# Twelve of sixteen token tiles transposed by VectorE and DRAM instead of TensorE, with the norm's gain folded into the gate's weights

## The chip, the cores and the metric

One core of one Trainium2 chip. The metric is the device time of one execution in microseconds, the median over the runs; lower is better. The kernel is a single launch on that core.

## What is computed

A pre-norm encoder layer over 2048 tokens of width 1024, in float32: an mLSTM mixer, a squared-ReLU MLP, then the part that this change touches, a gated per-token embedding, and a last norm.

```python
h = h + mix                                            # mLSTM mixer
h = h + sqrelu_mlp(rmsnorm(h, norm_mlp[i]), mlp_w1[i], mlp_w2[i])
gate = sigmoid(rmsnorm(h, norm_ple[i]) @ ple_gate_w[i] + ple_gate_b[i])
h = h + gate * (p[i] @ ple_w[i])                       # p: 2048 x 256
return rmsnorm(h, norm_final)

def rmsnorm(x, gain):
    return x * rsqrt(mean(x * x, axis=-1) + EPS) * gain
```

The norm's gain multiplies columns of h, so it may as well multiply rows of the gate's weights; the reciprocal root is one number per token, so it may as well multiply the gate's product afterwards.

## The kernel before

A product in float32 is made of three matmuls: each operand is split into a rounded part (`hi`, type fp32r) and the rest (`lo`), and `mm3` adds hi*hi, hi*lo and lo*hi in one PSUM bank. ScalarE makes `hi` by a cast, VectorE makes `lo` by a subtraction (`split`). The weights are split once, by `Weight.prep`.

The mixer and the MLP's two products fill the first 2170 us (the MLP by seven products in place of eight on 2x2 blocks; banks `pa`, `pb`, `pc`). The MLP's second product adds its results to the residual `h1_d` in DRAM by accumulating DMAs on POOL's queue. The last part takes the 2048 tokens as 16 tiles of 128, numbered 0 to 15 here. For each tile `Tok`:

- `load` brings the tile's 128x1024 residual (`h2`) on SP's queue, four tiles ahead. The residuals of tiles 2 and up lie in a ring of seven buffers (`Ot`), so the load of tile t+7 waits until tile t has been written out.
- `norm` sums squares on ScalarE, makes the reciprocal root (`rstd`: ScalarE's log and exp, then one Newton step of VectorE) and scales the tile by it and by the gain's row `row_ple` (VectorE, 128x1024, result `xs`).
- `tr0` and `tr1` transpose half a tile each: four 128x128 transposes on TensorE into the one PSUM bank `pt`, then `split` into `xTh` and `xTl`.
- `half` does half of the output columns, twice: 24 gate matmuls into `pg` (8 blocks of the width, three each), 6 matmuls of the embedding into `pl`, then bias, sigmoid, product, residual add and sum of squares.
- `fin` makes the last norm and writes the tile out, on POOL's queue (the last two tiles on SP's and ScalarE's).

The embedding `p` already takes another way to its transposed form, before the last part: VectorE transposes 32x32 blocks (`shuffle`), four POOL DMAs write the blocks to DRAM in an order (`p_d`) from which one SP load (`shuffled`) gives whole transposed tiles. The same helper served the mixer (`mix_d`) and the MLP (`mlp_d`).

Each engine runs its instructions in the order written; that order is made by a scheduler from the program's order (the loop over tiles at the end, and the lists `late` that put the preparations beside the MLP's last products). Every instruction that goes through the recording wrapper has line L100 in the profile, whatever its place in the code, so groups are told apart by tile names; the profile leaves buffer numbers out and shows `h2` as `h`.

Of the kernel before, what the change touches and what calls it, by code (L numbers as in the profile page):

```python
# [8 lines left out]
F32 = mybir.dt.float32  # L9
F32R = mybir.dt.float32r  # L10
AF = mybir.ActivationFunctionType
ALU = mybir.AluOpType
# [4 lines left out]
P = 128  # L17
S = 2048
D = 1024
KD = D // P  # L20
NC = S // P
# [14 lines left out]
def hybrid_mlstm_kernel(  # L36
# [72 lines left out]
    V, A, G, TE, SP = Engine(nc.vector), Engine(nc.scalar), nc.gpsimd, Engine(nc.tensor), nc.sync  # L109
# [24 lines left out]
    make_identity(nc, ident)  # L134
    ones = const.tile([P, P], F32, name="ones")
    G.memset(ones, 1.0)
    gains = {nm: const.tile([P, KD], F32, name=f"g_{nm}") for nm in ("mix", "hn")}

    def gain_load(nm, g):
        SP.dma_start(gains[nm], g.rearrange("(k p) -> p k", p=P))  # L140
# [24 lines left out]
    def split(hi, lo, src, eng=None):  # L165
        A.copy(hi, src)
        (eng or V).tensor_tensor(lo, src, hi.bitcast(F32), op=ALU.subtract)

    def rstd(ss, n):
# [9 lines left out]
        V.tensor_tensor(y, y, t, op=ALU.mult)  # L179
        return y  # L180

    def small(nm, bufs=3):
        return sb.tile([P, 8], F32, tag=nm, bufs=bufs, name=nm)
# [6 lines left out]
    class Weight:  # L190
# [11 lines left out]
                SP.dma_start(self.st[..., at:at + n], src)  # L202
                at += n

        def prep(self, eng=None):
            self.hi = Ht("whi", self.shape, F32R)
            self.lo = Ht("wlo", self.shape, F32R)
            split(self.hi, self.lo, self.st, eng)
            self.st = None

    def cols_w(w, c0, n=P):
# [145 lines left out]
    class Early(Prep):  # L357
# [957 lines left out]
    class Early_p:  # L1315
# [21 lines left out]
        def split(self):  # L1337
            self.hi, self.lo = Ht("pTh", [P, 2, 512], F32R), Ht("pTl", [P, 2, 512], F32R)
            split(self.hi, self.lo, self.z)

    class Tok:
        def __init__(self, t, pt):
            self.t, self.pt = t, pt

        def load(self):
            self.h2 = (Ht if self.t < 2 else Ot)("h2", [P, D])
            SP.dma_start(self.h2, ple_rows(h1_d, self.t))

        def norm(self):
            xs, ss = Ht("xs", [P, D]), small("ss1")  # L1350
            A.activation(xs, self.h2, AF.Square, scale=1.0 / 32.0, accum_out=ss[:, 0:1])
            r = rstd(ss[:, :1], 1)
            V.scalar_tensor_tensor(xs, self.h2, r[:, 0:1], rowc["ple"], op0=ALU.mult, op1=ALU.mult)
            self.xs = xs

        def tr(self, i):
            if i == 0:
                self.hi, self.lo = Ht("xTh", [P, KD, P], F32R), Ht("xTl", [P, KD, P], F32R)
            pt, ks = ps_s("pt"), slice(4 * i, 4 * i + 4)
            for k in range(4):  # L1360
                TE.transpose(pt[:, k * P:(k + 1) * P], self.xs[:, (4 * i + k) * P:(4 * i + k + 1) * P], ident)
            split(self.hi[:, ks], self.lo[:, ks], pt.rearrange("p (k t) -> p k t", t=P))

        tr0, tr1 = (lambda self: self.tr(0)), (lambda self: self.tr(1))
# [7 lines left out]
        def half(self, n, gate=True):  # L1372

            if n == 0:
                self.ss = small("ssf")
            if gate:
                self.gate(n)
            sl, pg = slice(n * 512, (n + 1) * 512), self.pg
            tk = slice((self.t % 4) * P, (self.t % 4 + 1) * P)
            pl = ps_tr("pl")  # L1380
            for k in range(2):
                mm3(pl, self.pt.hi[:, k, tk], self.pt.lo[:, k, tk], wpl[k].hi[:, sl], wpl[k].lo[:, sl], k == 0, k == 1)
            g, h = St("g", [P, 512]), self.h2[:, sl]
            V.tensor_tensor(g, pg, rowc["gb"][:, sl], op=ALU.add)
            act(g, g, AF.Sigmoid)
            V.tensor_tensor(g, pl, g, op=ALU.mult)
            V.tensor_tensor(h, g, h, op=ALU.add)
            A.activation(g, h, AF.Square, scale=1.0 / 32.0, accum_out=self.ss[:, n:n + 1])
# [170 lines left out]
    def row_load(nm, src):  # L1559
        rowc[nm] = Ht(f"row_{nm}", [P, D])  # L1560
        SP.dma_start(rowc[nm], src.partition_broadcast(P))
# [67 lines left out]
        up[1][-1].side += pr.preps()  # L1629

    pp = [Early_p(t) for t in (0, 4, 8, 12)]
    toks = [Tok(t, pp[t // 4]) for t in range(NC)]
    for g in range(4):
        down[16 + 4 * g].side.append(pp[g].dma)
        down[18 + 4 * g].side.append(pp[g].put)
    late = {41: [wgt[0].dma, wgt[1].dma, lambda: row_load("ple", norm_ple[0])],
            42: [wgt[0].prep, wgt[1].prep, wgt[2].dma, toks[0].load],
            43: [wgt[2].prep, wgt[3].dma, wgt[4].dma, toks[1].load, toks[0].norm],
            44: [wgt[3].prep, wgt[4].prep, wgt[5].dma, toks[2].load, lambda: row_load("gb", gate_b[0])],
            45: [wgt[5].prep, wgt[6].dma, wgt[7].dma, pp[0].get, toks[1].norm, toks[3].load],  # L1640
            46: [wgt[6].prep, wgt[7].prep, toks[0].tr0, pp[0].split],
            47: [wpl[0].dma, wpl[1].dma, toks[0].tr1, lambda: row_load("nf", norm_final)]}
    for s, fs in late.items():
        down[s].side += fs
    run7(up[0] + up[1] + down)
# [2 lines left out]
    for t in range(NC):  # L1648
        nx = toks[t + 1] if t + 1 < NC else None
        if nx:  # L1650
            nx.tr0()
        if t == 0:
            toks[t].gate(0)
            pg0 = toks[t].pg
            nx.tr1()
            toks[t].gate(1)
            pg1 = toks[t].pg
            wpl[0].prep()
            wpl[1].prep()
            toks[t].pg = pg0  # L1660
        toks[t].half(0, t > 0)
        if t + 4 < NC:
            toks[t + 4].load()
        if nx and t > 0:
            nx.tr1()
        if t % 4 == 2 and t + 2 < NC:
            pp[t // 4 + 1].split()
        if t % 4 == 0 and t + 4 < NC:
            pp[t // 4 + 1].get()
        if t == 0:  # L1670
            toks[t].pg = pg1
        toks[t].half(1, t > 0)
        if t > 0:
            toks[t - 1].fin()
        if t + 2 < NC:
            toks[t + 2].norm()
    toks[NC - 1].fin()


# [20 lines left out]
```

## Time and profile before

| | |
|---|---|
| median of 3 runs | 2426.96 us (2424.62 to 2428.15) |
| the profiled execution: its own time | 2426.04 us |
| its span, first to last instruction | 2424.3 us |
| TensorE busy | 2375.9 us (98%) |
| VectorE / ScalarE / POOL busy | 65% / 48% / 25% |
| granted TensorE clock, mean | 0.997 |
| last part, first gate matmul to the end | 2166.9 to 2424.3 us |

A matmul of 512 columns is shown with 0.39 us, but matmuls overlap: one begins every 0.23 us. So TensorE's pace is read from starts, not from durations. The bracket at the end of a row is idle time before it and what ended it.

### The profile page before, as it was taken

What the parts mean: (1) busy time and instruction counts of PE and PEld (TensorE: products, weight loads), DVE (VectorE), ACT (ScalarE), POOL (GpSimd) and SP (SyncE); (2) the same over time, 40 slices, a digit from 0 to 9 for tenths busy, and PEclk for the clock granted to TensorE, in tenths of its full rate; (3) what the DMA queues carried; (4) which work ended last, traced back from release to release, by engine and by line L of the source; (5) the groups of instructions that cost most, each with busy time, mean ns of one, the idle gap of its engine ahead of it and who ended that gap; (6) DMA issues with size and microseconds to landing.
All of it is one profiled execution on the core that took longest, in us unless ns stands there. A gap on an engine that the chain in (4) does not pass through costs nothing.

```text
span 2424.3 us, 31650 instructions
## 1 busy us (share of the span) xinstructions
PE 2375.9 (98%) x11317; PEld 1958.0 (81%) x11317; DVE 1573.3 (65%) x2601; ACT 1163.7 (48%) x2166; POOL 601.8 (25%) x633
## 2 busy tenths in 40 slices
PE   7999999999999999999999999999999999999998
PEld 6988888787889987888888888787887888887776
DVE  6667545557777887667674444866676767656665
ACT  5245424436788874433343333544443444445554
POOL 1041122124333324446543333011111111110000
PEclk9999999999999999999999999999999999999999
DMA  5676656867768873457573321667677776892211
GB/s 171 230 214 203 190 143 221 288 220 279 239 218 287 287 261 116 133 160 224 193 233 114 110 96 61 185 148 165 153 184 173 175 161 156 192 229 86 78 56 48
DMA packets 264501, 429.11 MB, mean 177 GB/s; under 512 B 46952, under 2 KB 174312, under 8 KB 264344
## 3 DMA queue, kind: packets, MB, share of 16 engines
q1 hardware_dynamic: 204376, 303.23, 38.2%
q0 software_dynamic: 59680, 123.35, 21.8%
q8 instruction: 88, 1.44, 0.2%
q14 instruction: 69, 0.57, 0.1%
q10 hardware_dynamic: 288, 0.52, 0.1%
HBM read 257.62 MB, written 169.21 MB: 176 GB/s over the span
## 4 chain that ended last, share of the span: by engine, by line
PE 77%; issue 8%; DVE 6%; DMA 4%; ACT 4%; POOL 1%; SPq 0%; DVEq 0%; ACTq 0%; POOLq 0%
PE pa L100 30%; PE pb L100 15%; PE pc L100 7%; PE psf L100 6%; PE pso L100 5%; PE pg L100 4%; PE psv L100 4%; PE pn L100 3%; PE pu L100 1%; PE pt L100 1%; PE pl L100 1%; ACT L100 1%; DMA hst<-hid_d 1%; DMA cb_d<-Clo 1%; DVE h L100 1%
## 5 line engine op out<-in xcount | busy, mean ns | idle before, releaser
L100 PE MATMUL pa<-op 128*128 128x512 f32 x3360 | 826.1, 395 | 6.6 <-ACT e L100 3.6
L100 PEld LDWEIGHTS pa<-op 128*128 128x128 f32 x3360 | 630.4, 188 | 159.0 <-ACT e L100 6.5
L100 PE MATMUL pb<-op 128*128 128x512 f32 x1632 | 407.8, 394 | 0.8 <-DVE op L100 0.8
L100 PEld LDWEIGHTS pb<-op 128*128 128x128 f32 x1632 | 306.2, 188 | 74.0 <-DVE op L100 1.1
L100 DVE TENSOR_TENSOR op<-sa,op 128x1024 fp32r<-128x1024 f32 (+2 forms) x176 | 188.7, 1078 | 147.4 <-ACT op L100 111.6
L100 ACT CAST op<-sa 128x1024 fp32r<-128x1024 f32 (+2 forms) x176 | 156.4, 895 | 167.6 <-PE pb L100 84.2
L1287 POOL DMA_DIRECT2D h_d<-o x96 | 93.1, 973 | 563.3 <-DVE o L100 494.1
L100 ACT COPY e<-pa 128x512 f32<-128x512 f32 x160 | 93.8, 587 | 262.1 <-PE pa L100 261.4
L100 PE MATMUL pc<-op 128*128 128x512 f32 x768 | 191.8, 394 | 0.1
L100 PEld LDWEIGHTS pc<-op 128*128 128x128 f32 x768 | 144.2, 188 | 34.5 <-DVE op L100 0.6
L100 PE MATMUL psv<-whi,xT 128*128 128x272 f32 (+2 forms) x720 | 161.7, 318 | 0.6 <-DVE xT L98 0.6
L100 PE MATMUL psf<-xT,whi 128*128 128x512 f32 x512 | 160.6, 394 | 0.0
L100 DVE TENSOR_TENSOR op<-wst,op 128x512 fp32r<-128x512 f32 x112 | 123.8, 1108 | 34.8 <-ACT op L100 22.0
L100 ACT CAST op<-wst 128x512 fp32r<-128x512 f32 x112 | 92.6, 834 | 108.5 <-DVE op L100 59.6
L100 PEld LDWEIGHTS psv<-whi,xT 128*128 128x128 f32 x720 | 118.9, 189 | 10.0 <-DVE xT L98 0.8
L461 POOL TENSOR_TENSOR sa<-wst 128x512 f32<-128x512 f32 x32 | 58.9, 1841 | 264.8 <-PE pb L100 168.5
L100 PE MATMUL psv<-wlo,xT 128*128 128x272 f32 (+2 forms) x360 | 114.1, 317 | 0.0
L100 PEld LDWEIGHTS psf<-xT,whi 128*128 128x128 f32 x512 | 95.2, 188 | 21.3
L100 PE MATMUL pso<-whi,hThi 128*128 128x512 f32 x256 | 102.1, 400 | 3.7 <-ACT nt L100 2.5
L100 PE MATMUL pg<-whi,xTl 128*128 128x512 f32 x256 | 101.9, 398 | 0.0
L100 PE MATMUL pg<-whi,xTh 128*128 128x512 f32 x256 | 101.1, 395 | 0.0
L100 PE MATMUL pg<-wlo,xTh 128*128 128x512 f32 x256 | 101.0, 394 | 0.0
(254 smaller groups left out, 4338.3 us busy)
## 6 DMA issues: line engine op xcount, KB each, us to landing
wst<-in_mlp_w SPq DMA_DIRECT2D x96, 512.0 KB
h_d<-o POOLq DMA_DIRECT2D x96, 512.0 KB, 12.4
hid_d<-e SPq DMA_DIRECT2D x128, 256.0 KB
hst<-hid_d SPq DMA_DIRECT2D x64, 384.0 KB
wst<-in_mlstm_w_in SPq DMA_DIRECT2D x44, 512.0 KB
vst<-v_d SPq DMA_DIRECT2D x31, 512.0 KB
raw<-in_x SPq DMA_DIRECT2D x16, 512.0 KB
kq<-kq_d SPq DMA_DIRECT2D x16, 512.0 KB
```

The costliest lines, as they stand in the source:

```text
L100: r = f(*a, **kw)
L461: eng.tensor_tensor(s[:, 0], r1[:, :, P:], r2[:, :, P:], op=add_)
L1287: G.dma_start(rows(h1_d, 2 * q + i), o[i], accum_op=add_)
```

## The change

Three things, all in the last part:

1. The gain `norm_ple` is loaded as a column (128x8, `g_ple`) during the MLP, and `prep` of the eight gate weights multiplies by it: ScalarE's cast becomes an activation with a scale, VectorE's subtraction becomes a scalar_tensor_tensor. The row `row_ple` (a load of 512 KB) goes.
2. `norm` now makes the reciprocal root only (kept in `rt`). The scaling of the tile (`xs`) goes; the transposed operand is the residual itself, and the root is applied where the bias is added (`tensor_tensor` becomes `scalar_tensor_tensor`).
3. For tiles 4 to 15, in six pairs, the transposes move: in the odd tile t of the loop, `put` transposes the residuals of tiles t+3 and t+4 by 32x32 blocks on VectorE (four instructions of 128x512) and writes them to DRAM by eight POOL DMAs of 128 KB, in pieces of 256 B; at the end of the next, even, tile `get` loads them back by two SP loads of 512 KB in pieces of 1 KB. `tr` then only splits, from SBUF rather than PSUM. Tiles 0 to 3 keep TensorE's transposes.

```diff
-            split(self.hi, self.lo, self.st, eng)
+            if gain is None:
+                split(self.hi, self.lo, self.st, eng)
+            else:
+                A.activation(self.hi, self.st, AF.Copy, scale=gain)
+                V.scalar_tensor_tensor(self.lo, self.st, gain, self.hi.bitcast(F32), op0=ALU.mult, op1=ALU.subtract)
...
+    class Early_h:
+        def __init__(self, t0):
+            self.d = dram.tile([32, 32, 4, 64], F32, name=f"h2{t0}_d")
+        def put(self, m, h2):
+            y = Ht("y", [P, 16, 2, 32])
+            for j in range(2):
+                V.transpose(y[:, :, j, :], h2[j][:, m * 512:(m + 1) * 512].rearrange("p (b i) -> p b i", i=32))
+            for q in range(4):
+                G.dma_start(self.d[16 * m:16 * m + 16, :, q].rearrange("b i e -> i b e"),
+                            y[32 * q:32 * q + 32].rearrange("i b j t -> i b (j t)"))
+        def get(self):
+            self.z = []
+            for m in range(2):
+                z = Ht("z", [P, 4, 256])
+                SP.dma_start(z, self.d[16 * m:16 * m + 16].rearrange("(k b) i q e -> (b i) k (q e)", b=4))
+                self.z.append(z.rearrange("p k (q j t) -> p j k q t", q=4, j=2))
...
         def norm(self):
-            xs, ss = Ht("xs", [P, D]), small("ss1")
-            A.activation(xs, self.h2, AF.Square, scale=1.0 / 32.0, accum_out=ss[:, 0:1])
-            r = rstd(ss[:, :1], 1)
-            V.scalar_tensor_tensor(xs, self.h2, r[:, 0:1], rowc["ple"], op0=ALU.mult, op1=ALU.mult)
-            self.xs = xs
+            ss, self.r = small("ss1"), small("rt", 4)[:, 0:1]
+            A.activation(Ht("jn", [P, D]), self.h2, AF.Square, scale=1.0 / 32.0, accum_out=ss[:, 0:1])
+            rstd(ss[:, :1], 1, self.r)
         def tr(self, i):
...
+            if self.e:
+                ks = slice(4 * i, 4 * i + 4)
+                hi, lo = (x_[:, ks].rearrange("p k (q t) -> p k q t", q=4) for x_ in (self.hi, self.lo))
+                split(hi, lo, self.e.z[i][:, self.t % 2])
+                return
             pt, ks = ps_s("pt"), slice(4 * i, 4 * i + 4)
             for k in range(4):
-                TE.transpose(pt[:, k * P:(k + 1) * P], self.xs[:, (4 * i + k) * P:(4 * i + k + 1) * P], ident)
+                TE.transpose(pt[:, k * P:(k + 1) * P], self.h2[:, (4 * i + k) * P:(4 * i + k + 1) * P], ident)
...
-            V.tensor_tensor(g, pg, rowc["gb"][:, sl], op=ALU.add)
+            V.scalar_tensor_tensor(g, pg, self.r, rowc["gb"][:, sl], op0=ALU.mult, op1=ALU.add)
...
+    down[30].side.append(lambda: gain_load("ple", norm_ple[0]))
...
+        if t % 2 and t + 4 < NC:
+            for m in range(2):
+                eh[t // 2 + 2].put(m, (toks[t + 3].h2, toks[t + 4].h2))
+        if t % 2 == 0 and t >= 2 and t + 2 < NC:
+            eh[t // 2 + 1].get()
```

TensorE, around the start of tile 10, before (`pg_20316` is the first gate half of tile 10, `xs_20292` the scaled tile 11):

```order
L100 MATMUL pg_20316<-whi_18955,xTl_20184 128x512
L100 MATMUL pl_20341<-whi_19133,pTh_19865 128x512
L100 MATMUL pt_20308<-ident_67,xs_20292 128x128 x4
L100 MATMUL pl_20341<-wlo_19134,pTh_19865 128x512
L100 MATMUL pl_20341<-whi_19133,pTl_19866 128x512
```

And now, from the end of the `pl` products that the order sets ahead of tile 10's gate (`pl_20479` is of tile 11; `pg_20333` and `pg_20379` are tile 10's two gate halves, `xTh_20201` and `xTl_20202` its transposed operand):

```order
L100 MATMUL pl_20479<-wlo_19144,pTh_19881 128x512
L100 MATMUL pl_20479<-whi_19143,pTl_19882 128x512
L100 MATMUL pg_20333<-whi_18562,xTh_20201 128x512
L100 MATMUL pg_20333<-wlo_18563,xTh_20201 128x512
L100 MATMUL pg_20379<-whi_18562,xTh_20201 128x512
L100 MATMUL pg_20379<-wlo_18563,xTh_20201 128x512
L100 MATMUL pg_20333<-whi_18562,xTl_20202 128x512
```

The four transposes of each half tile are gone from this place. Tiles 10, 12 and 14 now have four groups of `pl` (the tile's before, the own two, the next tile's first) before their gate, and their two gate halves are interleaved.

VectorE, at the end of tile 9, before (`h2_19608` is tile 8, `h2_19983` tile 11):

```order
L100 TENSOR_TENSOR ssf_20192<-ssf_20192 128x1
L100 SCALAR_TENSOR_TENSOR h2_19608<-h2_19608,rsy_20280,row_nf_19049 128x1024
L100 TENSOR_TENSOR rst_20297<-rsa_20295,rsy_20296 128x1
L100 TENSOR_SCALAR rsa_20406<-ssf_20192 128x1
L100 TENSOR_TENSOR rst_20297<-rst_20297,rsy_20296 128x1
L100 TENSOR_SCALAR rst_20297<-rst_20297 128x1
L100 TENSOR_TENSOR rsy_20296<-rsy_20296,rst_20297 128x1
L100 SCALAR_TENSOR_TENSOR xs_20292<-h2_19983,rsy_20296,row_ple_18476 128x1024
```

And now (`h2_19631` is tile 8, `h2_20125` and `h2_20244` are tiles 12 and 13, `z_20197` and `z_20199` the first and second half of the loaded pair 10 and 11):

```order
L100 SCALAR_TENSOR_TENSOR h2_19631<-h2_19631,rsy_20288,row_nf_19055 128x1024
L100 TENSOR_TENSOR xTl_20202<-z_20197,xTh_20201 128x512
L100 STREAM_TRANSPOSE y_20314<-h2_20125 128x16x32
L100 TENSOR_SCALAR rsa_20304<-ss1_20300 128x1
L100 STREAM_TRANSPOSE y_20314<-h2_20244 128x16x32
L100 TENSOR_TENSOR rst_20306<-rsa_20304,rsy_20305 128x1
L100 STREAM_TRANSPOSE y_20321<-h2_20125 128x16x32
L100 TENSOR_TENSOR rst_20306<-rst_20306,rsy_20305 128x1
L100 STREAM_TRANSPOSE y_20321<-h2_20244 128x16x32
L100 TENSOR_SCALAR rst_20306<-rst_20306 128x1
L100 TENSOR_TENSOR xTl_20329<-z_20197,xTh_20328 128x512
L100 TENSOR_TENSOR xTl_20202<-z_20199,xTh_20201 128x512
```

The transposes of pair 12 and 13 stand behind the first subtraction of pair 10 and 11, and ahead of the second.

POOL's queue, which before held one output in each tile, now (`h210_d` holds pair 10 and 11, `h2_19378` is tile 6, `h2_19504` tile 7):

```order
L1358 DMA h210_d_9395<-y_20068 32x16x64 x2
L1429 DMA out_0<-h2_19378 128x1024
L1358 DMA h210_d_9395<-y_20068 32x16x64 x2
L1358 DMA h210_d_9395<-y_20075 32x16x64 x4
L1429 DMA out_0<-h2_19504 128x1024
```

Six of the pair's eight writes stand behind the output of tile 6.

## Rows read from the trace of the kernel before

**Rows 1.** The page: busy time, share of the span and instructions of each engine; and the TensorE clock that was granted, in tenths of full speed, in 40 equal slices of the span.

```profile
PE 2375.9 (98%) x11317; PEld 1958.0 (81%) x11317; DVE 1573.3 (65%) x2601; ACT 1163.7 (48%) x2166; POOL 601.8 (25%) x633
...
PEclk9999999999999999999999999999999999999999
```

**Rows 2.** Busy time of each engine in a stretch of 50 us of the last part (us; in brackets instructions), then granted clock, share of the DMA engines and GB/s.

```profile
2250.00:2300.00 50.00, 49.16 (x226) 38.85 (x225) 32.29 (x73) 25.20 (x51) 2.13 (x4) 1.00 0.24 84
```

**Rows 3.** TensorE's instructions in order of time through one tile of the last part, from the first `pl` matmul of one tile to that of the next: start, duration, engine, line, operation and tiles.

```profile
2252.87 0.40 PE L100 MATMUL pl<-whi,pTh 128*128 128x512 f32 x1
2253.40 0.63 PE L100 MATMUL pt<-ident,xs 128*128 128x128 f32 x4
...
2254.10 0.39 PE L100 MATMUL pl<-whi,pTl 128*128 128x512 f32 x1
...
2255.25 0.39 PE L100 MATMUL pg<-wlo,xTh 128*128 128x512 f32 x1
2255.48 0.61 PE L100 MATMUL pt<-ident,xs 128*128 128x128 f32 x4
...
2256.16 0.40 PE L100 MATMUL pg<-whi,xTh 128*128 128x512 f32 x1
...
2267.97 0.40 PE L100 MATMUL pl<-whi,pTh 128*128 128x512 f32 x1
```

**Rows 4.** The chain of work that ended last, in order of time: tile 15, which has no transposes of a following tile beside it (start, us, what).

```profile
2397.73 1.39 PE pl L100 x6
2399.12 5.57 PE pg L100 x24
2404.70 1.40 PE pl L100 x6
2406.09 5.55 PE pg L100 x24
```

**Rows 5.** POOL in order of time: the first and the last of the 14 outputs on its queue.

```profile
2206.17 0.62 POOL L1399 DMA_DIRECT2D out<-h  x1 [25.79 <-DVE rst L100]
...
2403.26 0.67 POOL L1399 DMA_DIRECT2D out<-h  x1 [14.48 <-DVE rsa L100]
```

**Rows 6.** TensorE in order of time at tile 1, with the idle time before the transposes in brackets.

```profile
2189.53 0.40 PE L100 MATMUL pg<-whi,xTl 128*128 128x512 f32 x1
2190.50 0.63 PE L100 MATMUL pt<-ident,xs 128*128 128x128 f32 x4 [0.58 <-DVE ssf L100]
```

**Rows 7.** Groups of VectorE in the last part, shapes apart: count, busy us and mean ns of one, idle time before and its releaser.

```profile
L100 DVE TENSOR_TENSOR xTl<-pt,xTh 128x512 fp32r<-128x512 f32 x32 | 22.0, 686 | 12.4 <-ACT xTh L100 12.4
...
L100 DVE SCALAR_TENSOR_TENSOR xs<-h,rsy,row_ple 128x1024 f32<-128x1024 f32 x14 | 18.0, 1285 | 0.7 <-DVE rsy L100 0.3
...
L100 DVE TENSOR_TENSOR wlo<-wst,whi 128x1024 fp32r<-128x1024 f32 x3 | 3.7, 1222 | 8.1 <-ACT whi L100 8.1
```

**Rows 8.** The cast of ScalarE in the last part, same columns.

```profile
L100 ACT CAST xTh<-pt 128x512 fp32r<-128x512 f32 x32 | 18.6, 580 | 55.5 <-PE pt L100 55.4
```

**Rows 9.** The instructions that write or read tile `y` of the earlier shuffles: count, then duration in ns (least, median, most), first and last start, shapes.

```profile
L100 DVE STREAM_TRANSPOSE y<-raw x64: 391/403/447, 158.6 to 1111.0; 128x256 f32<-128x256 f32 x64
```

**Rows 10.** Instructions with the mixer's gain: a split from a loaded `z`, read in runs of 32 elements, and the same from PSUM (`pt`).

```profile
L100 ACT ACTIVATE xT<-z,g_mix x16: 708/715/727, 255.7 to 282.2; 128x512 fp32r<-128x512 f32 x16
L100 DVE SCALAR_TENSOR_TENSOR xT<-z,g_mix,xT x16: 740/744/752, 256.5 to 283.1; 128x512 fp32r<-128x512 f32 x16
...
L100 DVE SCALAR_TENSOR_TENSOR xT<-pt,g_mix,xT x8: 743/750/752, 41.3 to 49.0; 128x512 fp32r<-128x512 f32 x8
```

**Rows 11.** POOL in order of time at 994 us: the MLP's eight shuffle writes, one behind the other.

```profile
994.26 4.67 POOL L341 DMA_DIRECT2D mlp_d<-y  x8 [6.91 <-DVE y L100]
```

**Rows 12.** DMA in the 10 us from there: the queue of POOL (packets, MB, share of 16 engines) and the issues by line (count, KB each, median us from issue to landing).

```profile
q0 software_dynamic: 384, 1.05, 48.8%
...
mlp_d<-y POOLq DMA_DIRECT2D x8, 128.0 KB, 4.0
```

**Rows 13.** DMA issues from 1962 to 1990 us, where the DMA engines are loaded: one set of four shuffle writes.

```profile
p_d<-y POOLq DMA_DIRECT2D x4, 128.0 KB, 14.4
```

**Rows 14.** DMA from 2200 to 2400 us: the two queues' shares of 16 engines, and the outputs.

```profile
q0 software_dynamic: 3792, 6.82, 10.4%
q1 hardware_dynamic: 1543, 5.01, 7.8%
...
out<-h POOLq DMA_DIRECT2D x13, 512.0 KB, 3.5
```

**Rows 15.** The chain of waits from 2150 to 2215 us: the longest DMA piece in it.

```profile
2167.61 13.36 DMA wst<-in_ple_w
```

**Rows 16.** VectorE in order of time after the last gate matmul of tile 15.

```profile
2411.67 0.69 DVE L100 TENSOR_TENSOR g<-pg,row_gb 128x512 f32<-128x512 f32 x1 [4.05 <-PE pg L100]
2413.12 0.69 DVE L100 TENSOR_TENSOR g<-pl,g 128x512 f32<-128x512 f32 x1 [0.77 <-ACT g L100]
...
2415.58 1.28 DVE L100 SCALAR_TENSOR_TENSOR h<-h,rsy,row_nf 128x1024 f32<-128x1024 f32 x1
```

**Rows 17.** What SP's queue waited for from 2100 us on: us in total, times, longest.

```profile
SPq L1347 <- DMA out<-h: 118.8, 7, 24.7
```

More of the change, by code (lines that the diff above doesn't have):

```diff
@@ L136, in hybrid_mlstm_kernel @@
     G.memset(ones, 1.0)
-    gains = {nm: const.tile([P, KD], F32, name=f"g_{nm}") for nm in ("mix", "hn")}
+    gains = {nm: const.tile([P, KD], F32, name=f"g_{nm}") for nm in ("mix", "hn", "ple")}
     def gain_load(nm, g):
@@ L167, in split, with rstd @@
         (eng or V).tensor_tensor(lo, src, hi.bitcast(F32), op=ALU.subtract)
-    def rstd(ss, n):
+    def rstd(ss, n, out=None):
         T = lambda nm: sb.tile([P, 8], F32, tag=nm, bufs=3, name=nm)[:, :n]
@@ L178, in rstd @@
         V.tensor_scalar(t, t, -0.5, 1.5, op0=ALU.mult, op1=ALU.add)
-        V.tensor_tensor(y, y, t, op=ALU.mult)
-        return y
+        out = y if out is None else out
+        V.tensor_tensor(out, y, t, op=ALU.mult)
+        return out
     def small(nm, bufs=3):
@@ L203, in dma, with prep @@
                 at += n
-        def prep(self, eng=None):
+        def prep(self, eng=None, gain=None):
             self.hi = Ht("whi", self.shape, F32R)
             self.lo = Ht("wlo", self.shape, F32R)
-            split(self.hi, self.lo, self.st, eng)
+            if gain is None:
[3 more added lines that the diff above has]
+                V.scalar_tensor_tensor(self.lo, self.st, gain, self.hi.bitcast(F32), op0=ALU.mult, op1=ALU.subtract)
             self.st = None
@@ L1339, in split, with __init__ @@
             split(self.hi, self.lo, self.z)
+    class Early_h:
[14 more added lines that the diff above has]
+                self.z.append(z.rearrange("p k (q j t) -> p j k q t", q=4, j=2))
     class Tok:
-        def __init__(self, t, pt):
-            self.t, self.pt = t, pt
+        def __init__(self, t, pt, e):
+            self.t, self.pt, self.e = t, pt, e
         def load(self):
@@ L1631, in hybrid_mlstm_kernel @@
     pp = [Early_p(t) for t in (0, 4, 8, 12)]
-    toks = [Tok(t, pp[t // 4]) for t in range(NC)]
+    eh = [None, None] + [Early_h(t) for t in range(4, NC, 2)]
+    toks = [Tok(t, pp[t // 4], eh[t // 2]) for t in range(NC)]
+    gp = [lambda k=k: wgt[k].prep(None, gains["ple"][:, k:k + 1]) for k in range(KD)]
     for g in range(4):
@@ L1635, in hybrid_mlstm_kernel @@
         down[18 + 4 * g].side.append(pp[g].put)
[L1636 to L1641, printed above, removed]
+    late = {41: [wgt[0].dma, wgt[1].dma],
+            42: [gp[0], gp[1], wgt[2].dma, toks[0].load],
+            43: [gp[2], wgt[3].dma, wgt[4].dma, toks[1].load, toks[0].norm],
+            44: [gp[3], gp[4], wgt[5].dma, toks[2].load, lambda: row_load("gb", gate_b[0])],
+            45: [gp[5], wgt[6].dma, wgt[7].dma, pp[0].get, toks[1].norm, toks[3].load],
+            46: [gp[6], gp[7], toks[0].tr0, pp[0].split],
             47: [wpl[0].dma, wpl[1].dma, toks[0].tr1, lambda: row_load("nf", norm_final)]}
+    down[30].side.append(lambda: gain_load("ple", norm_ple[0]))
     for s, fs in late.items():
@@ L1660, in hybrid_mlstm_kernel @@
             toks[t].pg = pg0
+        g, i = t // 4 + 1, t % 4
         toks[t].half(0, t > 0)
@@ L1665, in hybrid_mlstm_kernel @@
             nx.tr1()
[L1666 to L1669, printed above, removed]
+        if i == 2 and t + 2 < NC:
+            pp[g].split()
+        if i == 0 and t + 4 < NC:
+            pp[g].get()
         if t == 0:
```

## The prediction

> **What bounds the kernel now.** I read the page first. TensorE is busy 98% of the span at a clock of 1.0 in nearly every slice [rows 1], so a matmul less is time less, if nothing else stops TensorE. The table by stretch says the same of the last part: 49.16 of 50 us busy, beside 32 of VectorE, 25 of ScalarE, 2 of POOL and a quarter of the DMA engines [rows 2]. All three resources that take the moved work have room. Then TensorE's order of time for one tile, to see what the transposes cost there. From the first `pl` matmul of one tile to that of the next are 15.10 us [rows 3]; from the first to the last output on POOL's queue 197.09 us for 13 tiles, 15.16 each [rows 5]. Tile 15, beside which no following tile is transposed, shows the bare work: half a tile from 2397.73 to 2404.70, 6.97 us, so 13.94 for a tile [rows 4]. The 1.2 us between can be seen in place: after the `pl` matmul at 2253.40 - 0.30 = 2253.10 another should have begun, and by 2254.10 only one had, 0.77 us lost, of which 0.30 was a wait for the scaled tile; after 2255.25, the matmul that should begin at 2255.71 begins at 2256.16, 0.45 lost [rows 3].
>
> **The change part by part.**
>
> *Transposes of tiles 4 to 15 leave TensorE.* 15.14 (between the two readings) less 13.94 is 1.20 us a tile, twelve tiles: **-14.4**. These are on the path, since TensorE waits for nothing else there.
>
> *The scaled tile goes.* Tiles 1 to 3 keep TensorE's transposes, but of the residual, which lies ready long before. Before, the transposes beside tile 1 waited: the matmul before began at 2189.53 and was followed at 2190.50, not at 2189.76, 0.74 us [rows 6]; the other two had some 0.30 each. At most 1.3 us; the least is nothing, if the release of the one transpose bank then comes last. I take **-0.9**, nearer the upper end since the scaling (1.285 us of VectorE) stood right ahead of the transposes.
>
> *Gain and root.* Eight subtractions of weights become scalar_tensor_tensor, 1.285 against 1.222 us [rows 7], 0.5 us of VectorE beside the MLP's last matmuls, where TensorE does not wait: nothing. Without that cover it would be these 0.5. The gain's column is a small load in place of one of 512 KB on SP's queue: nothing. The bias add with a root is some 0.06 longer, and only the last one is on the path: **+0.1**.
>
> *What VectorE gets.* Per pair it loses two scalings (2.6 us) and gets four transposes of 128x512. The trace has 128x256 only, 0.403 us [rows 9]; the nearest larger step is a subtraction, 0.686 for 512 and 1.222 for 1024 columns [rows 7], so twice the length costs a little less than twice: about 0.7 us, between 0.4 (no longer than half the size) and 1.5 (almost four times it). Splitting from SBUF in runs of 32 elements costs what splitting from PSUM does: 0.744 against 0.750 us on VectorE for the same form with a gain [rows 10]. On ScalarE that form takes 0.715 [rows 10] where the cast from PSUM took 0.580 [rows 8]; 0.14 us more in a list that is idle half the time, taken as nothing.
>
> *A new wait: the order.* VectorE's and ScalarE's lists now put the pair's splits behind the end of the tile before, and the next pair's transposes between them. I walk tile 10, with time 0 at the end of tile 9's last gate matmul. From tile 15, which has the same tail: bias add 0.03, product at +1.5, last norm's scaling from +3.9 to +5.2 [rows 4, 16]. So the first half's subtraction ends at +5.9, just when TensorE has done four `pl` groups of 1.39 (+5.6) and four matmuls of 0.23 (+6.5): no wait. Up to the second half's subtraction stand four transposes (2.8), five one-column instructions (0.9) and a subtraction (0.7): it ends at +11. TensorE has 17 matmuls until then (+10.4). So 0.5 us of waiting in tiles 10 and 12; tile 8 has a like order with the same four transposes, 0.5; tile 14 has none, since no pair follows. **+1.5**, between 0 and, with transposes of 1.5 us, 1.5 + 3 x 3.2 = 11.
>
> *A new wait: the way through DRAM.* Pair 12 and 13, from its first transpose at +5.9. The first half's two transposes take 1.6, four issues half of 4.67 [rows 11], landing 4.0 [rows 12], the load some 3.5, an estimate from an output of the same 512 KB in this part [rows 14]: 11.4 us. For the second half all eight issues count: 1.6 + 4.67 + 4.0 + 3.5 = 13.8. They are wanted two tiles later: the first about 4.7 us into tile 12, that is 27.9 + 4.7 - 5.9 = 26.7 us after the first transpose, the second about 9, 31 us after. For pair 10 and 11 six writes stand behind the output of tile 6, which waits for VectorE some 6 us longer: 20. So no wait. Loads of residuals on SP's queue stand behind outputs already (118.8 us in 7 waits [rows 17]), and are issued two tiles before they are transposed. **0**; the upper bound is the second rival.
>
> The eight 512 B-piece writes at 994 us took 48.8% of 16 engines for 10 us, 4.9 us of all of them [rows 12]; the new ones move the same bytes in twice the pieces. By bytes that is 4.9 us for each pair, by a fixed time for each piece 9.8. The Trainium skill (DMA: Bandwidth & Descriptors, Specifications) speaks against these pieces: line rate needs 512 B, below that the engine reads, changes and writes back. No row here shows it. If that doubled a piece's time, the writes would take 19.5 us; the way would be 1.6 + 19.5 + 4.0 + 3.5 = 28.6, still under 31, and the sum the same.
>
> Sum: -14.4 - 0.9 + 0.1 + 1.5 = **-13.7 us**. On the profiled execution's 2426.04 (span 2424.3 and 1.7 around it) that is 2412.3; it lay 0.9 below the median of 2426.96, from which I forecast **2413.3 us**.
>
> **The rivals.**
>
> *VectorE's list holds TensorE up (0.13).* If the transposes are 1.5 us each or the splits stand worse than I read, tiles 8, 10 and 12 lose 3.2 us more each: -13.7 + 9.7 = -4.0, 2423; half of that gives 2418. For it: the second half's split stands behind all four. Against it: the half-size row, and VectorE idle a third of the time.
>
> *The way through DRAM is late, and slower is the result (0.13).* Its place is the wait of tiles 10, 12 and 14 for their second half; VectorE's transposes of the next pair stand behind the first split of this one, so a pair's delay is handed on and not made up. Prices from the loaded stretches: landing 14.4 [rows 13], a load 13.4 [rows 15], issues of twice the length for twice the pieces, 9.3: 1.6 + 9.3 + 14.4 + 13.4 = 38.7, 7.7 late, three times 23: +9.4, 2436. It eats the whole gain from 31 + 13.7/3 = 35.6 us on. For it: the order itself puts three tiles' `pl` work ahead of these gates, as if the operand came late, and the piece size. Against it: those two rows are of stretches with the DMA engines loaded most of the time, while here queue shares add up to 18% [rows 14].
>
> *Nothing happens (0.04).* If the transposes were hidden, the time stays at 2427. Against it: tile 15's bare 13.94.
>
> **How the numbers follow.** The forecast holds with 0.70, and alone would range from 2411 to 2416 (the bounds of the second and the fifth part). About 0.2%, 4.9 us, is what a measurement of this kernel tells from no change. Faster by more than that: the forecast, and nearly all of the first rival, 0.82. Within: the rest of it, nothing happening, and a way that is late by 3 to 6 us for each pair, 0.10. Slower: a way later than that, 0.08. The range goes from 2410.5 (no waits at all, and half a microsecond of scatter) to 2421.5 (most of the first rival).
>
> **What would show it.** Right: outputs on POOL about 13.9 us apart from tile 4 on, with one gap of half a microsecond at tiles 8, 10 and 12; transposes `y<-h` of 0.7 us; TensorE at over 99% of the stretches there. Wrong: TensorE idle at tiles 8, 10, 12 or 14 by microseconds, with ScalarE's cast released by DMA `z` (the way is late) or by VectorE alone (the list); or a tile's period still over 15.

## The result, and the profile after

The changed kernel takes **2411.89 us** (median of 4 runs, 2410.42 to 2413.62) against 2425.79 (4 runs, 2423.89 to 2428.15): a ratio of 0.9943, 95% interval [0.9925, 0.996], 13.9 us less. Run again beside the experiments below (the first of them), it took 2411.49 (5 runs) against 2426.95 (17 runs): 0.9936 [0.9923, 0.9948], 15.5 us less. The forecast was 2413.3, with 13.7 less.

The profiled execution of the changed kernel lasted 2413.62 us with a span of 2411.9. Its page, against [rows 1]:

```profile
PE 2365.6 (98%) x11221; PEld 1953.1 (81%) x11221; DVE 1566.2 (65%) x2609; ACT 1162.8 (48%) x2166; POOL 631.6 (26%) x681
...
PEclk9999999999999999999999999999999999999999
```

TensorE has 96 instructions fewer, the eight transposes of twelve tiles, and its clock is as before. VectorE has 24 transposes more and 16 scalings fewer, and its total is 7 us lower. POOL has 48 more DMA issues and 30 us more.

Busy time by stretch, with the granted clock, the share of the DMA engines and GB/s at the end of a row. The second row answers to [rows 2]:

```profile
2200.00:2250.00 50.00, 50.00 (x222) 40.66 (x221) 30.57 (x74) 28.32 (x58) 8.83 (x14) 1.00 0.43 130
2250.00:2300.00 50.00, 50.00 (x217) 40.11 (x217) 33.47 (x81) 28.40 (x56) 11.23 (x18) 1.00 0.47 135
2300.00:2350.00 50.00, 50.00 (x217) 40.56 (x216) 32.11 (x76) 28.14 (x59) 9.18 (x15) 1.00 0.56 141
2350.00:2400.00 50.00, 49.82 (x215) 39.95 (x213) 28.66 (x67) 26.29 (x51) 7.22 (x11) 1.00 0.35 81
```

TensorE has no hole left. What was added is the DMA share: 0.47 in the stretch of [rows 2], where it was 0.24.

TensorE in order of time through one tile without transposes, from its first `pl` matmul to the next tile's, which answers to [rows 3]:

```profile
2231.31 0.39 PE L100 MATMUL pl<-whi,pTh 128*128 128x512 f32 x1
...
2245.19 0.40 PE L100 MATMUL pl<-whi,pTh 128*128 128x512 f32 x1
```

13.88 us, where the old kernel had 15.10. (Tile 1's part of the code reached this place 3 us later than in the old kernel's profile: 2189.27 against 2186.3. The MLP ahead of it lost them, and not because of the change: in the repeat's profile it came at 2184.86. Stretches are therefore compared from the first `pl` matmul on, 2186.50 here, and not on the clock of the span.)

From the first `pl` matmul to the last one the old kernel needs 229.11 us (2183.52 to 2412.63), the changed one 212.92 (2186.50 to 2399.42), the repeat 212.90. **The last part is 16.2 us shorter.** Two profiles of the changed kernel agree in this number to 0.02 us, while the four medians of the kernel before lie some 3 us apart, so the experiments are read by both.

### The profile page after: what moved, and what is told of

It reads as the page before. It is cut to its first block, busy times and chain, and to the rows that moved or that the text cites. A ratio compares the mean times of both kernels' runs of the same rounds, so it can differ in the third digit from the quotient of the medians.

```text
span 2411.9 us, 31565 instructions
## 1 busy us (share of the span) xinstructions
PE 2365.6 (98%) x11221; PEld 1953.1 (81%) x11221; DVE 1566.2 (65%) x2609; ACT 1162.8 (48%) x2166; POOL 631.6 (26%) x681
## 4 chain that ended last, share of the span: by engine, by line
PE 57%; DVE 2%; DMA 1%; issue 1%; ACT 1%; POOL 0%; DVEq 0%; ACTq 0%; POOLq 0%
PE pa L100 27%; PE pb L100 13%; PE pg L100 7%; PE pc L100 7%; PE pl L100 2%; DVE op L100 1%; DMA hst<-hid_d 1%; DMA wst<-in_mlp_w 1%; DVE raw L100 0%; ACT op L100 0%; DVE e L100 0%; DVE z L100 0%; DMA z<-tz_d 0%; PE pt L100 0%; ACT e L100 0%
## 5 line engine op out<-in xcount | busy, mean ns | idle before, releaser
L100 DVE TENSOR_TENSOR op<-hst,op 128x384 fp32r<-128x384 f32 (+1 forms) x96 | 65.4, 688 | 57.5 <-ACT op L100 37.2
L100 PE MATMUL psf<-xT,wlo 128*128 128x512 f32 x256 | 101.0, 394 | 0.0
```

The lines of the kernel that those rows point to most:

```text
L100: r = f(*a, **kw)
```

## The experiments

The theory after these rows: the sum is as forecast (fold and transposes), the list of VectorE costs next to nothing, and the way through DRAM is longer than reckoned but hidden. Rivals: the gain is the fold alone; VectorE's list is nearly full; the way is short and far from mattering, or long and just hidden. "Last part" is first to last `pl` matmul in the run's profile.

| run | median, us | before, us | ratio, 95% | last part, us |
|---|---|---|---|---|
| the kernel before (its profile) | | | | 229.11 |
| c_after: the change again | 2411.49 | 2426.95 | 0.9936 [0.9923, 0.9948] | 212.90 |
| e1: fold alone | 2421.13 | 2426.95 | 0.9981 [0.997, 0.9992] | 223.69 |
| e2: transposes kept on TensorE as well | 2420.28 | 2426.95 | 0.9979 [0.9969, 0.9988] | 223.66 |
| e3: put one tile later | 2444.38 | 2426.95 | 1.0071 [1.0055, 1.0086] | 247.73 |
| e4: writes twice, pieces of 256 B | 2417.28 | 2423.81 | 0.9974 [0.9961, 0.9987] | 219.88 |
| e5: the extra writes in pieces of 512 B | 2419.25 | 2423.81 | 0.9976 [0.9967, 0.9986] | 219.77 |
| e6: e3 with late outputs in four pieces | 2417.53 | 2423.81 | 0.9969 [0.9954, 0.9985] | 220.26 |
| e7: e3 with late outputs on SP | 2462.85 | 2423.81 | 1.0151 [1.0134, 1.0168] | 266.35 |
| e8: the change with late outputs in four pieces | 2414.96 | 2424.67 | 0.9958 [0.9945, 0.9972] | 214.78 |
| e9: the change with transposes twice | 2411.38 | 2424.67 | 0.9946 [0.9933, 0.996] | 214.26 |

**The change again.** Expected:

> The changed kernel once more. Every theory: 2412 us, 13.9 less than the kernel before. What it tells apart is where the profiled execution of the changed kernel lost some 3 us ahead of the last part (it reached tile 1 at 2189.3 us, the kernel before at 2186.3): if that is chance in the MLP, whose code did not change, this profile reaches tile 1 at another time, between 2184 and 2190; if the moved preparations cost it, again near 2189.

The median agrees within half a microsecond, and the last part within 0.02. The profile reached tile 1 4.4 us sooner than the first one, so those microseconds of the MLP are scatter.

**The fold alone (e1).**

```diff
-    eh = [None, None] + [Early_h(t) for t in range(4, NC, 2)]
+    eh = [None] * (NC // 2)
...
-        if t % 2 and t + 4 < NC:
-            for m in range(2):
-                eh[t // 2 + 2].put(m, (toks[t + 3].h2, toks[t + 4].h2))
-        if t % 2 == 0 and t >= 2 and t + 2 < NC:
-            eh[t // 2 + 1].get()
```

> Only the fold: gain in the gate's weights, root at the bias add, and all 16 tiles transposed by TensorE from the residual. Theory that the scaled tile's wait was part of the price of a tile (0.30 us for each of tiles 2 to 15, 0.74 at tile 1): -4.9 us, 2420.9; a tile's period 14.83. Rival, that the wait for the scaled tile hid another (the one transpose bank): no change, 2425.8, period 15.13.

TensorE in order of time, the transposes of two tiles, one period apart:

```profile
2253.88 0.60 PE L100 MATMUL pt<-ident,h 128*128 128x128 f32 x4
...
2268.68 0.60 PE L100 MATMUL pt<-ident,h 128*128 128x128 f32 x4
```

14.80 us for a tile, with transposes but with no wait ahead of them: the bracket of [rows 6] is gone. The fold alone gives 5.4 us of the last part (229.11 - 223.69), and 0.0019 of the whole, 4.6 us. The other 10.8 us (223.69 - 212.90) are the move's.

**The transposes kept as well (e2).** The changed kernel, and TensorE transposes tiles 4 to 15 besides, into a bank that nothing reads.

```diff
             if self.e:
...
                 split(hi, lo, self.e.z[i][:, self.t % 2])
+                pt = ps_s("pt")
+                for k in range(4):
+                    TE.transpose(pt[:, k * P:(k + 1) * P], self.h2[:, (4 * i + k) * P:(4 * i + k + 1) * P], ident)
                 return
```

> The changed kernel, with the transposes of tiles 4 to 15 left on TensorE as well, into a bank that nobody reads (24 groups of four). Theory that TensorE's time is the whole gain and the moved work is free: 24 x 0.45 = 10.8 us back, 2422.7, within 2 us of the fold alone. Rival, that the moved work on VectorE, POOL and DMA costs time of its own that the shorter list hides: 2 to 5 us above the fold alone. Rival, that only waits for the scaled tile were gained: no change against the changed kernel, 2412.

The last part is 223.66, that of the fold alone to 0.03 us. So 24 groups of four transposes cost 10.76 us of TensorE, 0.45 each, and everything that took their place (VectorE's transposes, 48 writes, 12 loads, the new order) costs the path nothing.

**The put one tile later (e3).** In the program the blocks go out at the end of the even tile, just ahead of the loads, instead of at the end of the odd tile before: one tile's time less for the way, 13.9 us. The scheduler took back a part of it: pair 12 and 13's first transpose came 143.6 us after the first `pl` matmul (2330.87 - 2187.24) against 134.3 in the changed kernel (2320.76 - 2186.50), 9.4 us later, and some 4 of these are the stalls of the tiles before.

```diff
-        if t % 2 and t + 4 < NC:
-            for m in range(2):
-                eh[t // 2 + 2].put(m, (toks[t + 3].h2, toks[t + 4].h2))
         if t % 2 == 0 and t >= 2 and t + 2 < NC:
+            for m in range(2):
+                eh[t // 2 + 1].put(m, (toks[t + 2].h2, toks[t + 3].h2))
             eh[t // 2 + 1].get()
```

> The way through DRAM begins one tile later: a pair's four transposes and eight writes stand at the end of the even tile, right ahead of its loads. The time left for the way falls by 13.9, from 31 us to 17. If the way takes 14 us, as worked out beforehand: no change, 2412. If it takes some 23 (in the changed kernel's profile the second load is issued 18 us after the first transpose, and 5 more to land): late by 6 for each of six pairs, +36, 2448, with TensorE idle ahead of tiles 4, 6, 8, 10, 12 and 14.

It lost more than all the gain, close to the longer of the two expected ways. But not as 6 us in each pair: tiles 4 to 10 lost 0.5 to 1.4, tile 12 lost 15.2, tile 14 lost 9.6. TensorE in order of time at tile 12:

```profile
2357.24 0.40 PE L100 MATMUL pg<-whi,xTl 128*128 128x512 f32 x1
2372.67 0.80 PE L100 MATMUL pg<-whi,xTh 128*128 128x512 f32 x1 [15.03 <-ACT xTh L100]
2373.27 0.63 PE L100 MATMUL pg<-wlo,xTh 128*128 128x512 f32 x1
2373.69 0.63 PE L100 MATMUL pg<-whi,xTl 128*128 128x512 f32 x1
```

The chain of waits leads from that cast back to POOL's queue (start, us, what):

```profile
2343.58 0.69 POOL out L1429
2344.27 1.08 POOL h_d L1358 x2
...
2346.20 9.90 DMA h_d<-y
...
2356.24 15.74 DMA z<-h_d
2371.98 0.02 issue
2372.00 0.63 ACT xTh L100
```

The second half's four writes stand behind an output on POOL's queue, take 9.9 us to land and are followed by a load of 15.7. From the pair's first transpose at 2330.87 to that landing at 2371.98 are 41 us. Tiles 4 to 10 go through the same steps without such times. What differs is the form of the output: tiles 8 to 15 lie in DRAM as four blocks of 32 rows (`by_quad`), so their outputs are DMAs of 4x32x1024 instead of 128x1024. The kernel before shows this already, with the DMA engines nearly idle. Issues from 2195 to 2250 us, tiles 0 to 2, and from 2360 to 2410, tiles 11 to 13 (count, KB, median us to landing):

```profile
out<-h POOLq DMA_DIRECT2D x3, 512.0 KB, 2.9
```

```profile
out<-h POOLq DMA_DIRECT2D x3, 512.0 KB, 10.3
```

The 3.5 of [rows 14] was a median over both kinds. In the changed kernel the pairs' writes follow them, 2195 to 2250 and 2310 to 2360:

```profile
h_d<-y POOLq DMA_DIRECT2D x16, 128.0 KB, 3.6
...
out<-h POOLq DMA_DIRECT2D x3, 512.0 KB, 3.0
```

```profile
h_d<-y POOLq DMA_DIRECT2D x16, 128.0 KB, 8.7
out<-h POOLq DMA_DIRECT2D x3, 512.0 KB, 11.2
```

**The late outputs in four pieces (e6).** e3, with one edit that leaves the order of the queue as it was:

```diff
-                if self.t < NC - 2:
+                if NC // 2 <= self.t < NC - 2:
+                    for i in range(4):
+                        G.dma_start(ple_rows(out_t, self.t)[i, :, sl], self.h2[32 * i:32 * i + 32, sl])
+                elif self.t < NC - 2:
                     G.dma_start(ple_rows(out_t, self.t)[..., sl], self.h2[:, sl])
```

> The late-put kernel (2444), in which tiles 12 and 14 lost 15.2 and 9.6 us, with the outputs of tiles 8 to 13 issued as four POOL DMAs of 32x1024 each in place of one of 4x32x1024; the order of the queue stays. In the traces those one-piece outputs land in 10.3 us, those of tiles 0 to 7 in 2.9, and the writes of pairs 10 to 14 stand beside or behind them and land in 8.7 to 9.9 us in place of 3.6 to 4.1. Theory (the long outputs make the way late): in four pieces they land in 3 to 5 us, the writes behind them in about 4, the stalls of tiles 12 and 14 fall to those of tiles 4 to 10 (0.5 to 1.5 us): 2415 to 2420. Rival (writes of 256 B or loads of 512 KB are slow by themselves when wanted one tile sooner): the stalls stay above 8 us each, 2438 or more. If the four pieces land no sooner than the one, 2444 again, and nothing is told apart.

From 2340 to 2372 us:

```profile
q0 software_dynamic: 816, 2.23, 28.3%
...
out<-h POOLq DMA_DIRECT2D x10, 128.0 KB, 2.5
h_d<-y POOLq DMA_DIRECT2D x9, 128.0 KB, 2.8
```

against, in e3:

```profile
q0 software_dynamic: 1440, 2.10, 29.8%
...
out<-h POOLq DMA_DIRECT2D x2, 512.0 KB, 12.9
h_d<-y POOLq DMA_DIRECT2D x8, 128.0 KB, 11.4
```

The stalls of tiles 12 and 14 are gone, those of tiles 4 to 10 stay (0.5, 1.4, 2.2 and 1.3), and 27.5 us of the last part come back. The way of pair 12 and 13 falls from 41 us to 23 (its first transpose at 2330.65, the last piece of its second load at 2353.92). So the way of the late pairs was long because of the form of the outputs beside them. It is not the bytes: POOL's queue moved 2.10 and 2.23 MB and held the DMA engines for 29.8% and 28.3%.

The kernel before shows what differs, in stretches where hardly anything else moves: tile 10's output in the late form, then tile 1's in the early one (the share of the DMA engines and GB/s stand last):

```profile
2359.00:2367.00 8.00, 7.84 (x39) 6.12 (x38) 3.74 (x7) 4.75 (x8) 0.00 (x0) 1.00 0.25 63
2222.40:2223.80 1.40, 1.26 (x8) 0.83 (x7) 1.17 (x2) 0.02 (x1) 0.00 (x0) 1.00 0.91 375
```

Both are 128 packets of 4 KB with data. The late form keeps a quarter of the DMA engines' time busy for eight microseconds, as if four of the sixteen carried it (an estimate from the 0.25); the early form keeps nearly all of them busy for little more than one. Which engines work, and why the form decides it, these traces do not show.

**The late outputs on SP (e7).** e3 with the outputs of tiles 8 to 13, in one piece, on the other queue.

```diff
-                    G.dma_start(ple_rows(out_t, self.t)[..., sl], self.h2[:, sl])
+                    (G if self.t < NC // 2 else SP).dma_start(ple_rows(out_t, self.t)[..., sl], self.h2[:, sl])
```

> The late-put kernel (2444) with the outputs of tiles 8 to 13 moved from POOL's queue to SP's, in one piece each as before. Then POOL's writes of pairs 10 to 14 stand behind no output and wait for none, while the loads of pairs 12 and 14 stand behind outputs on SP. Theory (what costs is the place behind an output on POOL's queue): writes start as soon as their blocks are transposed, the stalls of tiles 12 and 14 fall below 5 us each, 2415 to 2425. If the long outputs slow the writes by sharing the DMA engines, whatever queue they are on, the writes still land in 8 to 10 us and the stalls stay: 2430 to 2444. A third way: the loads, now behind outputs that wait for VectorE, come late instead, and tile 14 loses as much as before.

The third way came, and larger than expected. SP's queue in order of time ahead of tile 10:

```profile
2322.87 0.61 SPq L1429 DMA_DIRECT2D out<-h  x1
2333.80 0.52 SPq L1374 DMA_DIRECT2D h<-h_d  x1
2334.54 0.36 SPq L1365 DMA_DIRECT2D z<-h_d  x1
```

The output of tile 8 takes 10.9 us on this queue too; the load of tile 15's residual waits for it, since it goes into the same buffer; and the pair's second load stands behind that one. The cast followed at 2345.63, and tile 10 lost 20.4 us, tiles 12 and 14 some 10 and 9. POOL's writes of pair 12 and 13 landed in 2.7 to 4.8, as theory had it, but the run says nothing for or against the place behind an output on POOL's queue, since it made a worse place on SP's.

**The writes twice (e4, e5).** Each write of a pair is issued ahead of the real one into a tensor that nothing reads, in e4 in the same pieces, in e5 with two neighbouring blocks in one piece of 512 B.

```diff
...
             for q in range(4):
+                G.dma_start(self.x[16 * m:16 * m + 16, :, q].rearrange("b i e -> i b e"),
+                            y[32 * q:32 * q + 32].rearrange("i b j t -> i b (j t)"))
                 G.dma_start(self.d[16 * m:16 * m + 16, :, q].rearrange("b i e -> i b e"),
```

```diff
...
+                G.dma_start(self.x[8 * m:8 * m + 8, :, q].rearrange("b i e -> i b e"),
+                            y[32 * q:32 * q + 32].rearrange("i (b c) j t -> i b (c j t)", c=2))
```

> The changed kernel, with each write of a pair's blocks issued twice: first to a tensor that nothing reads, in the same pieces of 256 B, then to the place that is loaded. So 16 POOL writes for each pair in place of 8, which makes the way through DRAM longer without touching VectorE's order. In the changed kernel the loads were issued 18 us after the first transpose of pair 12 and 13, some 23 us with the load itself, and 31 are to be had. If a write of 128 KB takes about 10.6 us of engine time, as worked out from the queue's share (25.4% of 16 engines from 2200 to 2400 us), 48 more of them bring the share to about 41%; if they were twice as dear, to 57%. Time: eight more issues take 5.2 us more; the pairs 4 to 8 stay inside their 31 us; for pairs 10 to 14, whose writes land in 8.7 us, the way comes out between 28 and 36 us, so 2412 (all hidden) to 2425 (three tiles late by up to 5 us each, the delay handed on). I expect 2415.

> The same as with the doubled writes, but the extra write puts its 128 KB down in pieces of 512 B instead of 256 B. If what a write takes goes by bytes, POOL's share is the same within 2 points (about 41%) and the time within 2 us of the run with pieces of 256 B. If pieces under 512 B cost double, the extra writes take half of what the others take: the share is 8 points lower than with pieces of 256 B and, where that run loses time, this one loses less.

POOL's queue from 2200 to 2400 us: the changed kernel, e4, e5.

```profile
q0 software_dynamic: 6391, 12.95, 25.4%
```

```profile
q0 software_dynamic: 8193, 18.84, 38.1%
```

```profile
q0 software_dynamic: 8200, 18.84, 35.0%
```

5.89 MB more, 45 of the 48 writes, take 12.7% of 16 engines for 200 us in pieces of 256 B, 406 us or 9.0 each; in pieces of 512 B 9.6%, 307 us or 6.8 each. Neither expectation for the shares holds: by the queue's share, pieces of half the size cost 1.3 times as much, not the same and not double. Both runs lost 7 us of the last part, but most of the waits that the profile names are not those expected, and e5, with the cheaper pieces, was not the quicker of the two. TensorE's waits in e4, then in e5:

```profile
PE pg L100 <- DVE xTl L100: 3.2, 4, 0.8
PE pg L100 <- ACT xTh L100: 0.8, 1, 0.8
```

```profile
PE pg L100 <- DVE xTl L100: 2.3, 3, 0.8
PE pg L100 <- ACT xTh L100: 1.9, 1, 1.9
```

The waits of tiles 4 to 10 are for VectorE alone. VectorE's list is that of the changed kernel's tile 10 (the second half's subtraction ends 9.7 us after the gate of the tile before, in e4's tile 8 as there), but the scheduler no longer interleaves the two gate halves: TensorE wants that subtraction 14 matmuls after its first, 8.9 us after that gate, in place of 10.4 or later. That is the first rival's wait, 0.8 a tile, brought in by a changed order, so these runs measure the way's slack badly. Only tile 12's wait, 0.8 and 1.9, is the way's: ScalarE's cast waits there for DMA `z`, 1.2 us in e4 and 2.2 in e5, and gets it 32.0 and 33.0 us after the pair's first transpose (2356.30 - 2324.32, 2357.05 - 2324.05).

**The transposes twice (e9).** The changed kernel, every transpose of VectorE issued twice in a row.

```diff
-            for j in range(2):
+            for j in (0, 0, 1, 1):
                 V.transpose(y[:, :, j, :], h2[j][:, m * 512:(m + 1) * 512].rearrange("p (b i) -> p b i", i=32))
```

> The changed kernel with every one of VectorE's transposes issued twice in a row, into the same place: 2.6 us more of VectorE for each pair, the DMAs as they were. It is the first rival of the prediction made real (transposes of twice the length; there 1.5 us each, 3.2 us for each of tiles 8, 10 and 12, 2423). In the changed kernel the second half's subtraction ended 9.0 us after the gate of the tile before, TensorE wants it at 10.4: 1.4 us of room, so 2.6 - 1.4 = 1.2 us late at each of the tiles that have transposes ahead of their second split, at most 5 of them: +4 to +6, 2416 to 2418. If the order leaves them their cover in another place, +0 to +2. If VectorE's list were tight everywhere, 24 transposes of 0.66 us would come back whole, +15.8, 2427.

From 2200 to 2400 us VectorE is busy 137.8 us instead of 124.8, and the last part is 1.4 us longer, 214.26, with one wait:

```profile
PE pg L100 <- DVE xTl L100: 0.8, 1, 0.8
```

Of 15.8 us of new work on VectorE 14.4 lie beside TensorE's, against 10 to 12 in the expectation's main case; it is its second case, 0 to 2 us, that came. The scheduler gave the copies other places; at tile 10, the one with the wait, it put a split between the fifth and the sixth transpose. (The 9.0 us in the expectation are the end of the subtraction ahead of the one that counts, which ends at 9.8: the room was 0.6, not 1.4, and the cost came out smaller all the same.)

**The change with late outputs in four pieces (e8).** The same edit as in e6, on the changed kernel.

> The changed kernel with the outputs of tiles 8 to 13 in four POOL DMAs of 32x1024 each instead of one of 4x32x1024. In the late-put kernel these four landed in 2.6 us against 10.3, and the stalls of tiles 12 and 14 went. Here nothing waits for the way through DRAM, so by the theory (what the long outputs add to the way is hidden behind the two tiles' lead) the time stays that of the changed kernel, a ratio of 0.994 within 0.0015 (2410 to 2415 beside a before of 2426), though the loads of pairs 10 to 14 are issued about 10 us sooner and land sooner. Rival: some 2 us faster than the changed kernel, if landing writes and outputs disturb TensorE or the end of the kernel in a way that the chain does not show.

The pairs' writes land in 3.7 us instead of 5.3, outputs in 2.7, and nothing is gained: 0.9958 against 0.9936 with overlapping intervals, the last part 1.9 us longer, of which 1.3 are one wait of tile 12 for VectorE. The way of pair 12 and 13 fell to 18.6 us (2322.42 to the last piece of its second load at 2341.00), from 28.4 in the changed kernel. So the long way is hidden there, and shortening it is worth nothing. No version ran faster than the changed kernel by more than the scatter.

## Why the prediction was right

*Transposes off TensorE, -14.4 at 1.20 a tile.* Two things were in this term. The transposes proper, 0.45 for a group of four, two groups in each of twelve tiles: 10.8, as the gap of the second group had it [rows 3]; e2 gives 10.76. And the wait for the scaled tile, which the first group's row showed as 0.30: e1's period of 14.80 against 15.15 (from the transposes at 2253.40 to the next tile's at 2268.55 in the kernel before) makes it 0.35.

*The scaled tile goes, -0.9 for tiles 1 to 3.* It was the upper end, or a little more: fold alone gives 5.4 us, and twelve tiles of 0.35 leave 1.2 for these three and the root together.

*Gain, root and bias add, +0.1.* The bias add takes 746 ns against 688. The preparation of the weights with the gain left no wait on TensorE.

*VectorE's transposes, 0.7 us.* From the changed kernel, shapes apart (count, busy us, mean ns, idle before):

```profile
L100 DVE STREAM_TRANSPOSE y<-h 128x512 f32<-128x512 f32 x24 | 16.1, 696 | 1.1 <-DMA h<-h_d 0.8 <-issue 0.3
L100 DVE TENSOR_TENSOR xTl<-z,xTh 128x512 fp32r<-128x512 f32 x24 | 16.0, 677 | 0.1
L100 ACT CAST xTh<-z 128x512 fp32r<-128x512 f32 x24 | 13.8, 608 | 0.0
```

0.70, and the split from SBUF in runs of 32 costs what the one from PSUM did [rows 7, 8].

*A new wait, the order, +1.5.* **This step was wrong**: only tile 8 lost anything, 0.2 us. The walk was right in kind and slow by 1.2 us. VectorE in order of time ahead of tile 10:

```profile
2320.16 0.69 DVE L100 TENSOR_TENSOR xTl<-z,xTh 128x512 fp32r<-128x512 f32 x1
2320.76 0.70 DVE L100 STREAM_TRANSPOSE y<-h 128x512 f32<-128x512 f32 x1
2321.39 0.11 DVE L100 TENSOR_SCALAR rsa<-ss 128x1 f32<-128x1 f32 x1
2321.42 0.70 DVE L100 STREAM_TRANSPOSE y<-h 128x512 f32<-128x512 f32 x1
...
2323.41 1.28 DVE L100 TENSOR_TENSOR xTl<-z,xTh 128x512 fp32r<-128x512 f32 x2
```

The first subtraction ends 5.9 us after tile 9's gate (2314.94), as walked. Then transposes begin 0.66 us apart, and a one-column instruction between them adds some 0.04 (0.59 to 0.63 apart without one), where I had added 0.9 for five of them. The second half's subtraction, the last of the two in the last row, ends at 9.8, not 11, and TensorE wants it at 10.4. e9 shows how little hung on the transposes' length; e4 and e5 show that the wait is real, 0.8 a tile, once TensorE's order wants the second half sooner.

*A new wait, the way through DRAM, 0.* The result is right, the reckoning of 14 us was not. POOL for pair 12 and 13:

```profile
2322.41 1.96 POOL L1358 DMA_DIRECT2D h_d<-y  x3 [1.18 <-DVE rst L100]
2324.54 2.57 POOL L1358 DMA_DIRECT2D h_d<-y  x4 [0.17 <-issue]
2332.00 0.65 POOL L1358 DMA_DIRECT2D h_d<-y  x1 [4.89 <-DMA out<-h]
```

and SP's loads:

```profile
2333.33 5.79 SPq L1365 DMA_DIRECT2D z<-h_d  x2
```

The second load is issued 18 us after the first transpose (2338.8 - 2320.8); I had 10.3. The landing of 4.0 held for the early pairs, 3.6, and not for the late, 8.7. The eighth write waited 4.9 us for an output, because a DMA of POOL waits for the one eight before it on that queue, whose semaphore it takes over (in the trace the output issued at 2320.53 and the write at 2332.00 carry the same one). The load was not 3.5 either: 7.7 to 15.7 in the chain of e3, 11.1 in e7. Here the trace has the two loads' 1024 pieces of 1 KB; SP's queue from 2349 to 2361 us shows the last of them:

```profile
q1 hardware_dynamic: 5, 0.00, 0.1%
```

The very last begins at 2349.16, 10.4 us after the issue; ScalarE's cast follows at 2349.68 and did not wait. So the way took 28.4 us (2349.16 - 2320.76), counted to the start of that piece, of 31: it cost nothing by some 2.5 us, where I had reckoned 17 to spare. That this term came out at 0 is in part luck. The row that misled me is [rows 14]: one median over two kinds of output. The chance of 0.13 for the second rival was not too high; e3 shows the rival at work, a way of 41 us where the lead is shorter, with the delay of one pair handed on to the next, since the second half of the next pair's transposes (2374.01) stands behind the late split (2372.65).

*The pieces of 256 B.* The Trainium skill (DMA: Bandwidth & Descriptors, Specifications) has line rate from 512 B on, and a read, change and write below. The pieces of 256 B are dearer, 9.0 against 6.8 us of engine time for 128 KB, so it points the right way; the doubling that I made of it is not what the runs show. That the 28.6 worked out with it lies near the 28.4 measured is chance: the time went into late landings and a long load.

*The sum.* -13.7 forecast, -13.9 and -15.5 in the medians, -16.2 in the last part. The forecast is 2.5 us short of the last part: 1.3 from the order wait that did not come, the rest nearly all from the scaled tile (0.35 for 0.30 in twelve tiles, 0.6; some 0.4 at tiles 1 to 3). That the first median came within 0.2 of it is in part the scatter of the MLP ahead.

## What to carry to other kernels

Look at the landing time of every transfer that shares a queue with a new one, kind by kind, before using a median: two forms of one output, 2.9 and 10.3 us, made one row of 3.5. Where work leaves a full engine for idle ones, the price is in the lead that the new way gets: two tiles hid a way of 28 us with 2.5 to spare, and a start one tile later in the program cost twice the gain. And extra work put in to measure a slack can change the scheduler's order on another engine, so that the run measures the new order instead.

## What was not expected of the hardware

- An output of 512 KB as 4x32x1024 in one DMA takes 10.3 us to land with the DMA engines otherwise nearly idle, on POOL's queue and on SP's alike (10.9), and has a quarter of them busy meanwhile; as four DMAs of 128 KB 2.6 each; as 128x1024 2.9, with nine tenths busy.
- A write of 128 KB in pieces of 256 B takes 1.3 times the engine time of one in pieces of 512 B, 9.0 us against 6.8, by the share of POOL's queue in e4 and e5.
- Instructions of one column between VectorE's transposes are nearly free: 0.66 us from start to start with one between them, 0.59 to 0.63 with none (e9 has both), though such an instruction alone is shown with 0.11 to 0.16.
- After e3's stall of 15 us TensorE went on at the lower of its two levels, 1.2 GHz: matmuls began 0.43 us apart in place of 0.23, twelve of them, some 2.5 us. The granted clock by stretch (third figure from the end), right after the stall and later; before the stall it was 1.00:

```profile
2373.00:2378.00 5.00, 5.00 (x13) 3.81 (x13) 2.40 (x8) 1.52 (x2) 0.66 (x1) 0.50 0.47 128
2380.00:2400.00 20.00, 20.00 (x88) 16.31 (x87) 11.62 (x28) 10.79 (x22) 2.63 (x4) 1.00 0.26 46
```
